# Even-layer residual tiles in the odd layer's buffers, normed rows loaded two steps ahead, and first gates between key pieces

## The chip, the cores and the metric

The kernel runs on one core of a Trainium2 chip. A core has a matrix engine (TensorE, PE in the profile), three engines for elementwise work (VectorE, ScalarE and GpSimd: DVE, ACT and POOL) and a queue engine (SyncE, SP) that here issues nearly all DMAs. Each runs its own list of instructions in order; an instruction starts when the semaphores that it waits for have been raised. The metric is the device time of one execution in microseconds. A time for a version is the median of its timed runs; the profile is of one further execution.

## The reference

The program is one inference step of a two-layer decoder over 2048 prompt tokens and 32 decode tokens (8 sequences of 4), with D = 1024. Layer 0 (even) runs HGRN2 heads and forgetting-attention heads side by side and ends in one output projection; layer 1 (odd) is a gated linear attention (GLA). Cut to the part that matters here:

```
x  = x + concat(o_a, o_b) @ w_out_even           # end of layer 0, residual add
h  = rmsnorm(x, norm_odd)                        # rows of layer 1
q, k, v, g, r = split(h @ w_in_odd)              # 512, 512, 1024, 1024, 16 columns
log_f = log_sigmoid(r @ w_gate + b_gate) / 16    # per key column
o, S  = gated_linear(q * 128**-0.5, k, v, log_f, S0)
x  = x + (head_rmsnorm(o) * silu(g)) @ w_out_odd
return rmsnorm(x, final_norm), ...
```

## The kernel before, in words

Products run in three f16 terms (high times high, high times low, low times high; `mm3`, L583 to L585), so that each f32 operand is first split in two f16 parts by the elementwise engines. The activations of one half of the tokens lie in one tile `act`; half 0 has 1024 prompt tokens and the 32 decode tokens (written 1024 or "few" in names), half 1 the other 1024.

The work of PE is a row of *units*, each a weight block of 256 columns times one half of the tokens. `phase_odd` (L1940) makes them: units 0 to 3 are the even layer's output projection on half 0, units 4 to 7 the same on half 1 (`out_units`, L1787); units 8 to 10 are the odd layer's values, query-and-key, and output gate of head 0 on half 0 (`odd_half`, L1824), and so on. `staged` (L1201) runs a unit and, between its pieces, fetches and splits the weights of the next three.

An out unit goes over token tiles of 128 in pairs (`proj_tm`, L596): 48 matmuls into one PSUM buffer `pt_o` (tag `pj`, three buffers), and then `ev` (L1796) loads the residual rows into a tile `xo` (L1802), adds them to the product on DVE (L1803) and stores the sum to the scratch tensor `x1d` (L1805). A name such as xo0112 means layer 0, half 1, column block 1, token tile 2.

The normed rows of the odd layer are made by `norm_store` (L510), tile by tile of 128 rows: load from `x1d` into `x1r` (L521), sum of squares on ACT (`nsq`, L527), a scale on DVE (`rst_n`, L406) and its power on POOL (`rsr_n`, L408), the gain on POOL (L529), the split in f16 parts on ACT and DVE (L534, L535), and the store to `xs` (L536). Half 0's rows are worked between the pieces of units 4 to 7 (`mux`, L2058: the two generators advance at a fixed ratio). Afterwards `norm_fetch` (L547) loads `xs` transposed into `act`, where the columns that unit 7 has read are free.

Buffers are named by a tag and handed round in turn, so a tile waits for the last use of the tile that had its buffer before. Those that matter (L1947 to L1952): `yr`, two, holds raw attention outputs and `x1r`; `c2`, four, is shared with `th` and holds `xo`, the squares `nsq` and small temporaries; `c4`, six, holds q, k, f and u of the odd layer and lies idle until unit 9; `v8`, two, holds the odd layer's values and lies idle until unit 8.

In unit 9 (`mk_qk`, L1884) three query pieces come first, then `gate` (L1888), which issues its three small matmuls `zC` (L1893, also tag `pj`) in one go with ACT and DVE work on each (L1895, L1896) and four operations on the whole row (L1898 to L1901), then three key pieces.

The order of each engine's list is not that of the code alone: the program is built by a scheduler that simulates a timeline and places each instruction where the simulation has it start, so that a moved load also moves its neighbours on DVE, ACT, POOL and SP.

Of the kernel before, what the change touches and what calls it, by code (L numbers as in the profile page):

```python
# [8 lines left out]
F32 = mybir.dt.float32  # L9
# [5 lines left out]
AF = mybir.ActivationFunctionType  # L15
# [4 lines left out]
P = 128  # L20
D = 1024
KT = D // P
T = 2048
HALF = 1024
DB, DS = 8, 4
TS = DB * DS
# [97 lines left out]
class Kern:  # L124
# [382 lines left out]
    def few_first(tiles):  # L507
        return tiles[8:] + tiles[:8]

    def norm_store(self, pool, hf, tiles, gain):  # L510


        nc = self.nc
        todo = self.few_first(self.ttiles(hf))
        fly = {}

        def load(x):
            c0, n = todo[x]
            fly[x] = [y[:n] for y in tiles(c0)]
            dc = T if c0 >= HALF else hf * HALF + c0  # L520
            nc.sync.dma_start(fly[x][0], self.x1d[dc : dc + n])  # L521

        def norm(x):
            (c0, n), xt = todo[x], fly[x][0]
            sq = pool.tile([P, D], BF16, tag="th", name=f"nsq{c0}")
            ss = pool.tile([P, 1], F32, tag="nss", name=f"nss{c0}")
            nc.scalar.activation(sq[:n], xt, AF.Square, accum_out=ss[:n])  # L527
            fly[x].append(self.rstd(pool, ss[:n], [n, 1], D, f"n{c0}"))
            nc.gpsimd.tensor_tensor(xt, xt, gain[:n], ALU.mult)  # L529

        def split(x):
            (c0, n), (xt, t, r) = todo[x], fly.pop(x)
            dc = T if c0 >= HALF else hf * HALF + c0
            nc.scalar.activation(t[:, 0], xt, AF.Copy, scale=r)  # L534
            nc.vector.scalar_tensor_tensor(t[:, 1], xt, r, t[:, 0], ALU.mult, ALU.subtract)  # L535
            nc.sync.dma_start(self.xs[dc : dc + n], t.rearrange("p x d -> p (x d)"))  # L536

        for x in range(len(todo) + 2):
            if x > 1:
                split(x - 2)  # L540
            if x < len(todo):
                load(x)
            if 0 < x <= len(todo):
                norm(x - 1)
            yield 1000

    def norm_fetch(self, act, hf):  # L547
# [1239 lines left out]
    def out_units(self, hf, layer, act, wpool, wp, pps, x2=None, done=None):  # L1787

        nc, i = self.nc, self.i
        w = i[("w_out_even", "w_out_odd")[layer]][0]  # L1790

        def mk(u):
            cs = slice(u * 256, (u + 1) * 256)
            undo = [self.kcol()] + ([self.kcol()] if layer == 0 and hf == 0 else [])

            def ev(ps, g, cnt, m):  # L1796
                c0 = self.ttiles(hf)[g][0]
                c = undo[-1 if m < P else 0][:m]
                if x2 is None:
                    t = wp.tile([P, 2, 256], F32, tag="c2", name=f"xo{layer}{hf}{u}{g}")  # L1800
                    src = self.rows(hf, c0, m * cnt, layer == 0)[:, cs].rearrange("(g p) d -> p g d", g=cnt)
                    nc.sync.dma_start(t[:m, :cnt], src)  # L1802
                    nc.vector.scalar_tensor_tensor(t[:m, :cnt], ps, c, t[:m, :cnt], ALU.mult, ALU.add)  # L1803
                    dst = self.rows(hf, c0, m * cnt, False)[:, cs].rearrange("(g p) d -> p g d", g=cnt)
                    nc.sync.dma_start(dst, t[:m, :cnt])  # L1805
                else:
                    for j in range(cnt):
                        d = x2[g + j][:m, cs]
                        nc.vector.scalar_tensor_tensor(d, ps[:, j], c, d, ALU.mult, ALU.add)
                        if done:  # L1810
                            done(u, g + j, x2[g + j], cs)
                        if layer == 0 and u == 3:
                            nc.sync.dma_start(self.rows(hf, c0 + j * P, m, False), x2[g + j][:m])

            return (self.half_unit(wpool, pps, w, [(u * 256, 256)], f"o{layer}{u}", f"o{layer}{hf}{u}",
                                   also=list(zip(undo, (self.sy[layer], self.sy[2]))),
                                   raw=("yr", 256) if (hf, layer, u) == (0, 0, 0) else ("wr", WU),
                                   scaler="pool" if (hf, layer, u) == (0, 0, 0) else None),
                    lambda W: self.proj_tm(pps, act, W, hf, ev, f"o{layer}{hf}{u}", pairs=not done or u < 3))

        return [mk(u) for u in range(4)]


    def odd_half(self, hf, act, wpool, wp, pps, S):  # L1824
        nc, i, o = self.nc, self.i, self.o
        w = i["w_in_odd"][0]
        n = self.ncols(hf)
        q, f, k, v, vs, sg = {}, {}, {}, {}, {}, {}
# [4 lines left out]
        def c4(nm):  # L1833
            return wp.tile([P, HALF + TS], F32, tag="c4", name=nm)

        def unit(n, h, run):
            nm, cols = self.odd_cols(h)[n]
            return (self.half_unit(wpool, pps, w, cols, f"{nm}{h}", f"{nm}{hf}{h}"), run)

        def undo(nm):  # L1840
            return self.scales[nm][:, 2:3]
# [42 lines left out]
        def mk_qk(h):  # L1884
            def run(W):
                nm = f"C{hf}{h}"

                def gate():  # L1888
                    f[h], u = c4("f" + nm), c4("u" + nm)
                    ff = f[h]  # L1890
                    for c0, m in self.segs(hf):
                        ps = pps.tile([P, 512], F32, tag="pj", name=f"z{nm}{c0}")
                        nc.tensor.matmul(ps[:, :m], self.wg[:, h * P : (h + 1) * P], rTs[0][:, c0 : c0 + m],  # L1893
                                         start=True, stop=True)
                        nc.scalar.activation(ff[:, c0 : c0 + m], ps[:, :m], AF.Abs, bias=self.bgla[:, h : h + 1])  # L1895
                        nc.vector.tensor_scalar(u[:, c0 : c0 + m], ps[:, :m], self.bgla[:, h : h + 1], 0.0,  # L1896
                                                ALU.add, ALU.min)
                    nc.scalar.activation(ff[:, :n], ff[:, :n], AF.Exp, scale=-1.0)  # L1898
                    nc.scalar.activation(ff[:, :n], ff[:, :n], AF.Ln, bias=1.0)
                    nc.vector.tensor_tensor(ff[:, :n], u[:, :n], ff[:, :n], ALU.subtract)  # L1900
                    nc.scalar.activation(ff[:, :n], ff[:, :n], AF.Exp, scale=1.0 / 16)  # L1901

                q[h], k[h] = c4("q" + nm), c4("k" + nm)
                c = undo(f"Cqk{h}")
                if hf == 0:
                    nc.vector.tensor_scalar(self.q_undo[h], c, SCALE, None, ALU.mult)
                yield from self.proj_fm(pps, act, W, 0, P, hf, lambda ps, c0, m: nc.scalar.activation(
                    q[h][:, c0 : c0 + m], ps, AF.Copy, scale=self.q_undo[h]), nm + "q")
                gate()
                yield Z_C  # L1910
                yield from self.proj_fm(pps, act, W, P, P, hf, lambda ps, c0, m: nc.scalar.activation(
                    k[h][:, c0 : c0 + m], ps, AF.Copy, scale=c), nm + "k")

            return unit(1, h, run)

        def mk_g(h):
# [23 lines left out]
    def phase_odd(self):  # L1940
        tc, nc, i, o = self.tc, self.nc, self.i, self.o
# [3 lines left out]
        with pool("act2", side="right") as ap, pool("w2", side="right") as w0, pool("yr2", side="right") as y0, \  # L1945
                ExitStack() as late:
            raws = Pool(None, {"wr": 3})  # L1947
            wpool = Pool(w0, {"w": 3}, Pool(y0, {"yr": 2}), raws)
            c2s = Pool(None, {"c2": OC2, "th": "c2"})
            wp = Pool(None, {"c4": OC4, "sam": 1, "pd": 1, "kt": 2, "y": OY, "vp": 2, "v8": 2, "vs": 2, "rT": 1,  # L1950
                            "ss": 2, "rs_t": 2, "rs_r": 2, "sg": 3, "rt": 3, "rh": 3, "nss": 2, "gn": 1}, c2s)
            pps = Pool(None, {"pj": 3, "gr": 2, "st": 1, "o": 2})  # L1952
            S = []
            act = self.alloc_act(ap)
# [39 lines left out]
            def load(pieces):  # L1994
                for p in pieces[:2]:
                    p[0]()
                return pieces

            def split(pieces, loaded=2):
                for j, p in enumerate(pieces):  # L2000
                    for step in p[(1 if j < loaded else 0):]:
                        step()
# [42 lines left out]
            grow = self.gain_row(wp.tile([P, D], F32, tag="gn", name="grow"), i["norm_odd"][0], self.sx_odd)  # L2045
# [4 lines left out]
            def prep(hf):  # L2050

                def tiles(c0):
                    t = wpool.tile([P, KT, 256], F32, tag="yr", name=f"x1r{hf}{c0}").rearrange("p k t -> p (k t)")
                    return t[:, :D], t[:, D:].bitcast(F16).rearrange("p (x d) -> p x d", x=2)

                return self.norm_store(wp, hf, tiles, grow)

            drain(mux(prep(0), 11500.0, dense(4, 8), 84000.0))  # L2058
            fetched(11)
            self.norm_fetch(act, 0)  # L2060
# [100 lines left out]
```

## Time and profile before

| | us |
|---|---|
| median of 3 timed runs | 2394.37 (2386.42 to 2399.36) |
| profiled execution, its own time | 2385.88 |
| span of the profiled execution | 2384.2 |
| PE busy | 2273.3 |
| DVE, ACT, POOL busy | 1397.2, 1092.9, 815.8 |

In the profile's rows a bracket such as `[3.54 <-DVE xo L1803]` gives the time that the engine stood idle before the row, and the instruction that ended the wait. `PEclk` in a table by stretches is the share of full clock that TensorE was granted. On the span's time axis units 0 to 7 lie between about 1306 and 1497 us, unit 9 begins in the stretch 1520 to 1540. Lines such as L1803 are lines of the kernel before; in the changed kernel the same instructions stand a few lines lower (L1803 is L1807, L1802 is L1806, L1805 is L1809).

### The profile page before, as it was taken

The numbers are of one execution on the slowest core, as the hardware profiler recorded it, in microseconds if no ns is written. First come the engines' busy times: TensorE is split into PE (matmuls) and PEld (weight loads), VectorE is DVE, ScalarE is ACT, GpSimd is POOL, SyncE is SP. The second block draws the span as 40 slices with busy tenths as digits, with TensorE's granted clock in tenths as the row PEclk, the third lists the DMA queues.
The fourth block names the chain that finished last, engine by engine and source line by source line (L and its number), as shares of the span: only waits on it lengthen the run. The fifth ranks groups of instructions, "written<-read, shape, count | busy, mean of one in ns | idle before, by whom it ended". The sixth has DMA issues, their size and how long they took to land. (4 is left out here: it accounts for less than half of the span.)

```text
span 2384.2 us, 58245 instructions
## 1 busy us (share of the span) xinstructions
PE 2273.3 (95%) x23124; PEld 1617.0 (68%) x23124; DVE 1397.2 (59%) x3231; ACT 1092.9 (46%) x2379; POOL 815.8 (34%) x858
## 2 busy tenths in 40 slices
PE   6999999999999999999999998999899999999998
PEld 5667667864655876655446887777677676666887
DVE  7566566536654638566767444266675655557554
ACT  5334343333333226556667443446545535545333
POOL 1233324112212325234456344043552422322223
PEclk9999999999999999999999999999999999999999
DMA  6221334764441266776874767623233431115453
GB/s 199 63 86 60 93 111 138 193 167 139 144 130 55 78 203 232 241 254 204 267 237 134 248 201 226 158 77 120 83 112 97 114 104 60 43 59 160 154 191 150
DMA packets 358003, 344.89 MB, mean 145 GB/s; under 512 B 90993, under 2 KB 300722, under 8 KB 357730
## 3 DMA queue, kind: packets, MB, share of 16 engines
q1 hardware_dynamic: 356226, 336.64, 46.2%
q8 instruction: 182, 2.98, 0.5%
q0 software_dynamic: 1504, 4.52, 0.5%
q14 instruction: 91, 0.75, 0.1%
HBM read 248.73 MB, written 79.63 MB: 138 GB/s over the span
## 5 line engine op out<-in xcount | busy, mean ns | idle before, releaser
L583 PE MATMUL pt_o<-w_o,act 128*128 128x256 f16 x1024 | 282.9, 276 | 11.6 <-DVE xo L1803 9.2
L585 PE MATMUL pt_o<-w_o,act 128*128 128x256 f16 x1024 | 283.0, 276 | 4.8 <-DVE act L1766 4.1
L584 PE MATMUL pt_o<-w_o,act 128*128 128x256 f16 x1024 | 282.9, 276 | 0.0
L583 PEld LDWEIGHTS <-act 128*128 128x128 f16 x2304 | 227.7, 99 | 40.2 <-DVE xo L1803 3.8
L584 PEld LDWEIGHTS <-act 128*128 128x128 f16 x2304 | 227.7, 99 | 38.1 <-issue 7.6
L585 PEld LDWEIGHTS <-act 128*128 128x128 f16 x2304 | 227.9, 99 | 37.3 <-DVE act L1766 5.0
L749 POOL TENSOR_TENSOR kA<-kA,fA 128x512 f32<-128x512 f32 (+1 forms) x56 | 78.9, 1409 | 191.3 <-PE gl_A L715 142.7
L583 PE MATMUL pt_Cv<-w_Cv,act 128*128 128x256 f16 (+1 forms) x512 | 141.4, 276 | 0.0
L584 PE MATMUL pt_Cv<-w_Cv,act 128*128 128x256 f16 (+1 forms) x512 | 141.4, 276 | 0.0
L585 PE MATMUL pt_Cv<-w_Cv,act 128*128 128x256 f16 (+1 forms) x512 | 141.2, 276 | 0.0
L749 POOL TENSOR_TENSOR kC<-kC,fC 128x512 f32<-128x512 f32 (+1 forms) x56 | 83.5, 1492 | 151.8 <-PE gl_C L715 100.4
L1374 ACT ACTIVATE L<-L,nm,kc 128x512 f32<-128x512 f32 (+3 forms) x160 | 118.2, 741 | 37.5 <-DVE nm L1372 33.4
L1382 POOL TENSOR_SCALAR L<-L,nm 128x512 f32<-128x512 f32 (+3 forms) x160 | 98.8, 631 | 63.0 <-DVE nm L1378 22.1
L1409 ACT ACTIVATE th<-pt 128x512 f16<-128x512 f32 (+3 forms) x159 | 80.4, 527 | 61.3 <-PE pt L1402 60.3
L1410 DVE TENSOR_TENSOR tl<-pt,th 128x512 f16<-128x512 f32 (+3 forms) x159 | 94.5, 609 | 21.4 <-ACT th L1409 20.4
L1402 PE MATMUL pt<-ident,L 128*128 128x128 f32 x544 | 91.3, 280 | 6.5 <-POOL L L1382 3.8
L1402 PEld LDWEIGHTS pt<-ident,L 128*128 128x128 f32 x544 | 67.0, 144 | 32.8 <-DVE tl L1410 8.9
L1526 PEld LDWEIGHTS pkt<-ident,pgcache_fox_k 128*128 128x128 f32 x512 | 57.5, 141 | 42.6 <-issue 25.1
L1526 PE MATMUL pkt<-ident,pgcache_fox_k 128*128 128x128 f32 x512 | 74.7, 278 | 7.4 <-DVE kts L1530 5.3
L1855 ACT ACTIVATE vC<-pt_Cv,kc 128x512 f32<-128x512 f32 (+1 forms) x40 | 23.9, 599 | 123.2 <-PE pt_Cv L585 123.2
L583 PE MATMUL pt_Av<-w_Ai,act 128*128 128x256 f16 x256 | 71.1, 278 | 0.5 <-ACT act L578 0.5
L584 PE MATMUL pt_Av<-w_Ai,act 128*128 128x256 f16 x256 | 70.9, 277 | 0.4 <-DVE w_Ai L349 0.4
(952 smaller groups left out, 6752.9 us busy)
## 6 DMA issues: line engine op xcount, KB each, us to landing
pgcache_fox_k<-in_cache_fox_k SPq DMA_DIRECT2D x128, 256.0 KB, 4.3
pgcache_fox_v<-in_cache_fox_v SPq DMA_DIRECT2D x128, 256.0 KB, 4.1
yr<-yT SPq DMA_DIRECT2D x16, 1024.0 KB, 6.9
x1d<-xo SPq DMA_DIRECT2D x48, 256.0 KB, 3.6
wr_Aqf<-in_w_in_even SPq DMA_DIRECT2D x64, 128.0 KB, 3.3
wr_o<-in_w_out_even SPq DMA_DIRECT2D x32, 256.0 KB, 6.1
xo<-in_x_prompt SPq DMA_DIRECT2D x32, 256.0 KB, 3.4
wr_Cv<-in_w_in_odd SPq DMA_DIRECT2D x32, 256.0 KB, 3.8
```

Source lines behind the costliest of these rows:

```text
L583: nc.tensor.matmul(ps, lh[0], rh[0], start=first, stop=False)
L584: nc.tensor.matmul(ps, lh[0], rh[1], start=False, stop=False)
L585: return nc.tensor.matmul(ps, lh[1], rh[0], start=False, stop=last)
L749: nc.gpsimd.tensor_tensor(kv[:, :, 0], kv[:, :, 0], t1.to_broadcast([P, nb, w]), ALU.mult)
L1374: self.last_exp = nc.scalar.activation(lt[:, :w], lt[:, :w], AF.Exp, bias=nm[:, 0:1], scale=ib, accum_out=nm[:, 2 + j : 3 + j])
L1382: nc.gpsimd.tensor_scalar(lt[:, :w], lt[:, :w], nm[:, 1:2], 2.0**14, ALU.mult, ALU.mult)
L1402: nc.tensor.transpose(pt[:, w : w + P], rows[b][s // 4][0][:, (s % 4) * P : (s % 4 + 1) * P], self.ident)
L1409: nc.scalar.activation(th[:, a:w], pt[:, a:w], AF.Copy),
L1410: nc.vector.tensor_tensor(tl[:, a:w], pt[:, a:w], th[:, a:w], ALU.subtract)))
L1526: nc.tensor.transpose(pk[:, j * P : (j + 1) * P], pgs[j][:, h * P : (h + 1) * P], self.ident)
L1855: r = nc.scalar.activation(v[h][:, g : g + cnt], ps[:, :, :256], AF.Copy, scale=c)
```

## The change

Three parts. (1) In `ev`, the residual tiles of layer 0 come from tag `c4` (six buffers) in place of `c2` (four, shared with `nsq`); those of layer 1 stay. (2) `norm_store` has a parameter `lead`, the number of steps by which a row tile's load runs ahead of its norm: 2 for half 0, 1 for half 1 (which is the old order). For half 0 every second row tile (128, 384, 640, 896) is taken from `v8` in place of `yr`, so that there are four buffers. (3) In `mk_qk` the gate of head 0 is a generator that yields between its segments, and its steps are taken between the key pieces; the other heads' gates run through at once, as before.

```diff
@@ norm_store @@
-        for x in range(len(todo) + 2):
-            if x > 1:
-                split(x - 2)
-            if x < len(todo):
-                load(x)
-            if 0 < x <= len(todo):
-                norm(x - 1)
+        for x in range(-lead, len(todo) + 1):
+            if x > 0:
+                split(x - 1)
+            if x + lead < len(todo):
+                load(x + lead)
+            if 0 <= x < len(todo):
+                norm(x)
             yield 1000
@@ out_units, ev @@
-                    t = wp.tile([P, 2, 256], F32, tag="c2", name=f"xo{layer}{hf}{u}{g}")
+                    if layer:
+                        t = wp.tile([P, 2, 256], F32, tag="c2", name=f"xo{layer}{hf}{u}{g}")
+                    else:
+                        t = wp.tile([P, HALF + TS], F32, tag="c4", name=f"xo{layer}{hf}{u}{g}")[:, :512].rearrange(
+                            "p (g d) -> p g d", g=2)
@@ mk_qk @@
-                    for c0, m in self.segs(hf):
+                    for x, (c0, m) in enumerate(self.segs(hf)):
+                        if x and h == 0:
+                            yield
...
-                gate()
+                gates = gate()
+                next(gates, None)
                 yield Z_C
-                yield from self.proj_fm(pps, act, W, P, P, hf, lambda ps, c0, m: nc.scalar.activation(
-                    k[h][:, c0 : c0 + m], ps, AF.Copy, scale=c), nm + "k")
+                for x in self.proj_fm(pps, act, W, P, P, hf, lambda ps, c0, m: nc.scalar.activation(
+                        k[h][:, c0 : c0 + m], ps, AF.Copy, scale=c), nm + "k"):
+                    next(gates, None)
+                    yield x
@@ phase_odd, prep @@
-                    t = wpool.tile([P, KT, 256], F32, tag="yr", name=f"x1r{hf}{c0}").rearrange("p k t -> p (k t)")
+                    p, tag = (wp, "v8") if hf == 0 and c0 // P % 2 else (wpool, "yr")
+                    t = p.tile([P, KT, 256], F32, tag=tag, name=f"x1r{hf}{c0}").rearrange("p k t -> p (k t)")
...
-                return self.norm_store(wp, hf, tiles, grow)
+                return self.norm_store(wp, hf, tiles, grow, 1 + (hf == 0))
```

How it moves instructions is shown at three places. First the list of DVE in units 5 and 6 (half 1). Here rst_n384 is the scale of row tile 384, x1r0384 its split, and xo0112 the add that empties a PSUM buffer of unit 5. Before:

```order
L406 TENSOR_SCALAR rst_n256_20865<-nss256_20863 128x1
L1803 SCALAR_TENSOR_TENSOR xo0110_20778<-pt_o0110_20729,kc_67,xo0110_20778 128x512
L535 SCALAR_TENSOR_TENSOR x1r0256_20794<-x1r0256_20794,rsr_n256_20867 128x1024
L406 TENSOR_SCALAR rst_n384_20943<-nss384_20941 128x1
L1803 SCALAR_TENSOR_TENSOR xo0112_20853<-pt_o0112_20804,kc_67,xo0112_20853 128x512
L535 SCALAR_TENSOR_TENSOR x1r0384_20860<-x1r0384_20860,rsr_n384_20945 128x1024
L1803 SCALAR_TENSOR_TENSOR xo0114_20919<-pt_o0114_20870,kc_67,xo0114_20919 128x512
L406 TENSOR_SCALAR rst_n512_21071<-nss512_21069 128x1
L1803 SCALAR_TENSOR_TENSOR xo0116_20997<-pt_o0116_20948,kc_67,xo0116_20997 128x512
```

And after, from the same xo0110 on:

```order
L1807 SCALAR_TENSOR_TENSOR xo0110_20767<-pt_o0110_20718,kc_67,xo0110_20767 128x512
L535 SCALAR_TENSOR_TENSOR x1r0384_20849<-x1r0384_20849,rsr_n384_21062 128x1024
L406 TENSOR_SCALAR rst_n640_21256<-nss640_21254 128x1
L535 SCALAR_TENSOR_TENSOR x1r0512_20927<-x1r0512_20927,rsr_n512_21128 128x1024
L1807 SCALAR_TENSOR_TENSOR xo0112_20842<-pt_o0112_20793,kc_67,xo0112_20842 128x512
L535 SCALAR_TENSOR_TENSOR x1r0640_21055<-x1r0640_21055,rsr_n640_21258 128x1024
L406 TENSOR_SCALAR rst_n768_21325<-nss768_21323 128x1
L1807 SCALAR_TENSOR_TENSOR xo0114_20908<-pt_o0114_20859,kc_67,xo0114_20908 128x512
L535 SCALAR_TENSOR_TENSOR x1r0768_21121<-x1r0768_21121,rsr_n768_21327 128x1024
L406 TENSOR_SCALAR rst_n896_21389<-nss896_21387 128x1
L1807 SCALAR_TENSOR_TENSOR xo0116_20986<-pt_o0116_20937,kc_67,xo0116_20986 128x512
```

The row tiles have moved forward by about three tiles against the adds: where 384 stood beside xo0112, now 512 and 640 do. In the whole list the row tiles 128 to 896 now end between xo0104 and xo0120 (unit 6); before, the last, x1r0896, stood behind xo0124.

Second, SP's list at the start of the out units. Here yr... are the raw attention outputs (1 MB each) that become `act`, wr_o... weights, xo0000 the first residual load. Before:

```order
L330 DMA wr_o001_19308<-in_w_out_even 128x2x256 x4
L1802 DMA xo0000_19398<-in_x_prompt 128x2x256
L1752 DMA yr000512_19313<-yT0_76 128x8x256
L330 DMA wr_o002_19402<-in_w_out_even 128x2x256 x4
L1802 DMA xo0002_19469<-in_x_prompt 128x2x256
L330 DMA wr_o003_19473<-in_w_out_even 128x2x256 x4
L1802 DMA xo0004_19527<-in_x_prompt 128x2x256
L1802 DMA xo0006_19593<-in_x_prompt 128x2x256
L1752 DMA yr000768_19325<-yT0_76 128x8x256
L1752 DMA yr0010240_19337<-yT0_76 128x8x32
```

After:

```order
L330 DMA wr_o002_19402<-in_w_out_even 128x2x256
L1752 DMA yr000512_19313<-yT0_76 128x8x256
L330 DMA wr_o002_19402<-in_w_out_even 128x2x256 x3
L330 DMA wr_o003_19473<-in_w_out_even 128x2x256 x4
L1752 DMA yr000768_19325<-yT0_76 128x8x256
L1752 DMA yr0010240_19337<-yT0_76 128x8x32
L1806 DMA xo0000_19398<-in_x_prompt 128x2x256
L1806 DMA xo0002_19469<-in_x_prompt 128x2x256
L1806 DMA xo0004_19527<-in_x_prompt 128x2x256
L1806 DMA xo0006_19593<-in_x_prompt 128x2x256
```

The first four residual loads have moved behind the last two loads of raw outputs; POOL's scaling of the norm's gain row (`grow`, L458) has likewise moved behind POOL's splits of those two.

Third, ACT's list in unit 9, its three kinds of rows for the query (qC00), the gate (fC00) and the key (kC00). Before:

```order
L1907 ACTIVATE qC00_21856<-pf_C00q704_21920,kc_67 128x352
L1895 ACTIVATE fC00_21957<-zC000_21959,bgla_766 128x352
L1895 ACTIVATE fC00_21957<-zC00352_21963,bgla_766 128x352
L1895 ACTIVATE fC00_21957<-zC00704_21967,bgla_766 128x352
L1898 ACTIVATE fC00_21957<-fC00_21957 128x1056
```

After:

```order
L1913 ACTIVATE qC00_21856<-pf_C00q704_21920,kc_67 128x352
L1901 ACTIVATE fC00_21957<-zC000_21959,bgla_766 128x352
L1918 ACTIVATE kC00_21857<-pf_C00k0_21963,kc_67 128x352
L1901 ACTIVATE fC00_21957<-zC00352_21989,bgla_766 128x352
L1918 ACTIVATE kC00_21857<-pf_C00k352_21993,kc_67 128x352
L1901 ACTIVATE fC00_21957<-zC00704_22019,bgla_766 128x352
L1904 ACTIVATE fC00_21957<-fC00_21957 128x1056
```

The gate's segments alternate with the key pieces, on PE as on ACT. The same is done in unit 21 (half 1, two segments). Elsewhere the lists stand as before.

More of the change, by code (lines that the diff above doesn't have):

```diff
@@ L508, in few_first, with norm_store @@
         return tiles[8:] + tiles[:8]
-    def norm_store(self, pool, hf, tiles, gain):
+    def norm_store(self, pool, hf, tiles, gain, lead):
         nc = self.nc
```

## The prediction, made before the changed kernel was run

> **What bounds the kernel now.** I read the table of engines first.
>
> ```profile
> span 2384.2 us, 58245 instructions
> PE 2273.3 (95%) x23124; PEld 1617.0 (68%) x23124; DVE 1397.2 (59%) x3231; ACT 1092.9 (46%) x2379; POOL 815.8 (34%) x858
> ```
>
> PE is the bound, so only its idle time and its clock can be won. Next, the table by stretches around the change (out units from 1306 to 1497, unit 9 from about 1525).
>
> ```profile
> core 0: us, PE busy (x) PEld busy (x) DVE busy (x) ACT busy (x) POOL busy (x), PEclk, DMA share, GB/s
> 1300.00:1340.00 40.00, 36.05 (x331) 30.64 (x330) 21.36 (x31) 26.62 (x50) 23.27 (x19) 0.96 0.96 300
> 1340.00:1440.00 100.00, 99.93 (x965) 88.44 (x963) 40.21 (x55) 38.97 (x62) 35.91 (x24) 1.00 0.68 210
> 1440.00:1460.00 20.00, 16.46 (x137) 13.87 (x135) 5.10 (x8) 6.56 (x10) 6.40 (x5) 0.91 0.66 221
> 1460.00:1480.00 20.00, 17.17 (x143) 14.60 (x141) 8.41 (x9) 6.16 (x9) 9.40 (x7) 0.91 0.80 264
> 1480.00:1500.00 20.00, 17.15 (x141) 14.46 (x140) 7.23 (x8) 3.41 (x5) 5.11 (x4) 0.91 0.91 201
> 1520.00:1540.00 20.00, 16.76 (x119) 10.40 (x119) 7.40 (x19) 15.48 (x26) 2.33 (x2) 0.94 0.36 119
> 1540.00:1560.00 20.00, 20.00 (x133) 12.97 (x131) 4.48 (x4) 9.14 (x15) 2.72 (x2) 0.98 0.20 53
> ```
>
> PE is full from 1340 to 1440; then three stretches of 20 us each lose about 3 us of work and 0.09 of the clock. The waits of PE from 1290 to 1560 name what they wait for (total, times, longest):
>
> ```profile
> PE pt_o L583 <- DVE xo L1803: 9.2, 3, 3.5
> PE zC L1893 <- ACT qC L1907: 2.6, 1, 2.6
> PE pt_o L583 <- ACT act L1762: 1.5, 1, 1.5
> PE pS_o L627 <- DVE sam_o L622: 1.1, 1, 1.1
> PE pt_o L585 <- POOL act L1763: 0.6, 1, 0.6
> PE pf_C00k L583 <- DVE uC L1896: 0.6, 1, 0.6
> ```
>
> The 9.2 us are the three losses: PE has no PSUM buffer until DVE has added a residual. Why DVE is late, the timeline of SP, ACT, DVE and PE shows at the first of them:
>
> ```profile
> 1435.59 0.39 SPq L521 DMA_DIRECT2D x1r<-x1d  x1
> 1442.14 1.06 ACT L527 ACTIVATE nsq<-x1r 128x1024 bf16<-128x1024 f32 x1 [3.72 <-DMA x1r<-x1d]
> 1443.32 0.15 DVE L406 TENSOR_SCALAR rst_n<-nss 128x1 f32<-128x1 f32 x1 [3.58 <-ACT nsq L527]
> 1443.43 0.75 DVE L1803 SCALAR_TENSOR_TENSOR xo<-pt_o,kc,xo 128x512 f32<-128x512 f32 x1
> 1444.24 0.28 PE L583 MATMUL pt_o<-w_o,act 128*128 128x256 f16 x1 [3.54 <-DVE xo L1803]
> ```
>
> The add stands behind rst_n384 in DVE's list, that waits for nsq, and nsq for the load of its row tile, which was issued only at 1435.59, when its buffer came free. The waits from 1400 to 1500 confirm whose load it is:
>
> ```profile
> ACT nsq L527 <- DMA x1r<-x1d: 18.9, 6, 5.0
> DVE xo L1803 <- PE pt_o L585: 7.9, 2, 4.5
> DVE xo L1803 <- DMA xo<-in_x_sample: 0.5, 1, 0.5
> SPq L1802 <- ACT nsq L527: 16.3, 7, 4.6
> ```
>
> The adds hardly ever wait for their own residual (0.5 us); the row tiles do wait for theirs (18.9). The residual loads do wait, for a buffer that nsq holds (16.3), but they land in time.
>
> **The cost part by part.** *Row tiles in four buffers.* The present rhythm of row tiles and of pairs:
>
> ```profile
> 1424.79 1.06 ACT L527 ACTIVATE nsq<-x1r 128x1024 bf16<-128x1024 f32 x1 [4.96 <-DMA x1r<-x1d]
> 1477.68 1.06 ACT L527 ACTIVATE nsq<-x1r 128x1024 bf16<-128x1024 f32 x1 [4.02 <-DMA x1r<-x1d]
> 1492.13 0.75 DVE L1803 SCALAR_TENSOR_TENSOR xo<-pt_o,kc,xo 128x512 f32<-128x512 f32 x1 [3.38 <-PE pt_o L585]
> 1497.37 0.75 DVE L1803 SCALAR_TENSOR_TENSOR xo<-pt_o,kc,xo 128x512 f32<-128x512 f32 x1 [4.49 <-PE pt_o L585]
> x1r<-x1d SPq DMA_DIRECT2D x10, 512.0 KB, 4.4
> xs<-x1r SPq DMA_DIRECT2D x8, 512.0 KB, 3.9
> L529 POOL TENSOR_TENSOR x1r<-x1r,grow 128x1024 f32<-128x1024 f32 (+1 forms) x9 | 21.6, 2400 | 40.0 <-ACT nsq L527 33.6 <-DMA xs<-x1r 6.5
> L408 POOL TENSOR_TENSOR rsr_n<-rst_n,mhalf 128x1 f32<-128x1 f32 (+1 forms) x9 | 6.4, 715 | 0.0
> ```
>
> From nsq of tile 128 (1424.79) to that of tile 896 (1477.68) are six tiles: 52.9/6 = 8.8 us per tile, so a buffer's turn is 2 × 8.8 = 17.6 us. Four buffers give 17.6/4 = 4.4 us. No engine forbids that: POOL, the fullest, has 2.40 + 0.72 = 3.1 us per tile. A pair of PE takes 1497.37 − 1492.13 = 5.24 us. In the new list of DVE seven tiles (128 to 896) end between xo0104 and xo0120, six pairs apart: 6 × 5.24 = 31.4 us, and PE can run two pairs ahead on its three buffers, 10.5 more: 41.9. Seven tiles at 4.4 take 30.8, so PE isn't held and the 9.2 us go. The row tiles then end before unit 7 begins; what is late next is nothing that I find before the transposes, which wait for PE itself.
>
> *The clock.* In the three stretches with a gap it is 0.91, so 0.09 × 20 = 1.8 us are lost in each; at 1.00 elsewhere. With the gaps gone I take these 5.4 us too. [...] The three waits sum to 9.2 with a longest of 3.5, so the other two average 2.85, and their stretches stand at 0.91 nevertheless: I go by the rows.
>
> *Residual tiles in c4.* Same DMAs, same adds: nothing on the path in 1400 to 1500, because the loads already land in time there; the cover is the 5.24 us per pair times several buffers. It frees `c2` for nsq. Two waits are new and covered: unit 8's values now follow row tiles in `v8`, and unit 9's q, k, f and u follow residuals in `c4`, both stored before PE reaches these units. It costs something only at the start, where the first four loads now stand behind two loads of raw outputs:
>
> ```profile
> 1310.02 1.22 SPq L1802 DMA_DIRECT2D xo<-in_x_prompt  x2
> 1311.56 2.86 SPq L1752 DMA_DIRECT2D yr<-yT  x2
> 1322.41 2.91 POOL L458 TENSOR_SCALAR grow<-grow,kc 128x1024 f32<-128x1024 f32 x1 [8.39 <-DMA grow<-in_norm_odd]
> 1325.30 3.69 POOL L1763 TENSOR_TENSOR act<-yr,act 128x512 f16<-128x512 f32 x4
> 1323.97 0.28 PE L583 MATMUL pt_o<-w_o,act 128*128 128x256 f16 x1 [1.51 <-ACT act L1762]
> ```
>
> PE is ready for its fourth pair at 1323.97 − 1.51 = 1322.5. The gain's row held POOL there, ahead of its splits of the last raw outputs (1325.30), for which PE waited three times: 1.5 + 1.1 + 0.6 = 3.2 us, and 0.04 × 40 = 1.6 of clock, 4.8 together. In the new lists four residual loads (1 MB at 300 GB/s, some 3 us) no longer precede the raw outputs, and grow stands behind the splits. Against it, the first residual can't be issued before the second raw load, 1311.56 + 2.86 = 1314.4 or a little sooner. Landing as the row tiles' loads do (4.4) it is there at 1318.8, in time; with twice that, 1323.2, the add ends 1.5 us after PE is ready, and behind it in DVE's list stand the next unit's weight splits, so that PE may wait as long again: I bound the loss at 3. Between −4.8 and +3 I take half the gain, 2.4.
>
> *Gate between key pieces.* PE waited 2.6 + 0.6 us in unit 9 because `zC` needs a PSUM buffer that the third query piece holds, and its evacuation on ACT stood behind a weight's scaling that waited for its DMA:
>
> ```profile
> 1534.31 0.72 ACT L354 ACTIVATE wr_Cv<-wr_Cv,kc 128x512 f32<-128x512 f32 x1 [1.15 <-DMA wr_Cv<-in_w_in_odd]
> PE pf_C10k L583 <- ACT qC L1907: 1.9, 1, 1.9
> ```
>
> Now one `zC` and a key piece come before that buffer is needed: 24 matmuls of 352 columns, by the pair's 48 of 256 in 5.24 us some 3.6 us. That covers the 2.6, and both waits go: 3.2. The clock's share is 0.06 × 20 + 0.02 × 20 = 1.6. The gate's operations on the whole row end two key pieces later, but the recurrence that reads them begins only after unit 10. The second row above is the same wait in unit 21; there other work of the scheduler moved too, so between 0 and 1.9 I take 1.
>
> Sum: 9.2 + 5.4 + 2.4 + 3.2 + 1.6 + 1.0 = 22.8 us. The profiled execution took 2385.9 (span 2384.2), which gives 2363; it was 8.5 us below the median of the runs shown, 2394.4, so for a median I expect 2394.4 − 22.8 = 2371.6.
>
> **Rivals.** All as medians.
> (a) *Two buffers in effect.* If the row tiles keep their 8.8 us, because SP takes loads and stores in order and each tile's load queues behind a store that waits for DVE, seven tiles take 61.6 against 41.9: 19.7 us lost, 14.6 now. With 4.8 won at unit 9 it is even, 2394. For it speaks that SP's list still alternates loads with waiting stores; against it, that 128 and 384 are now loaded ahead of tile 1024.
> (b) *Slower.* The same mechanism with longer landings: more row and residual loads are in flight together where DMA already moves 201 to 264 GB/s. If load and store land 2 us later each, a two-buffer turn is 21.6 us, a tile 10.8, seven take 75.6: 33.7 lost, 19.1 more than now, 14 after unit 9's gain: 2409. It decides above 8.8 us per tile.
> (c) *The clock falls for another reason than gaps that short.* Then the clock's share of two of the three gaps, of unit 9 and half of that of the start stays: 1.8 + 1.8 + 1.6 + 0.8 = 6, and the time is 2378. Against it is that the stretches below 1.00 lie at gaps and the full one has none. [...]
>
> **How the numbers follow.** The forecast has 0.72. At the best the start gives 4.8 and unit 21 1.9, 3.3 us more than taken; at the worst the start costs 3 and unit 21 gives nothing, 6.4 less; with some 5 us either way, since the three runs spread over 13, its own range is 2363 to 2383. (a) has 0.13, (b) 0.07, (c) 0.08. The range begins at 2362 and reaches up to 2387, which takes in (c) and the part of (a) where some of the gain comes. What a measurement can tell from no change is about 0.5%, 12 us: faster is below 2382.4. That holds for nearly all of the forecast and (c), 0.77; (a) with the weak ends of both gives 0.15 for the same; (b) and a little of (a) 0.08 for slower.
>
> **What would show it.** Right: no wait of pt_o for xo from 1400 to 1490, PEclk 1.00 there, nsq about 4 to 5 us apart with few waits for x1r's load, zC without a wait, units 0 to 7 some 15 us shorter. Wrong: nsq still 8 to 9 us apart; pt_o waiting for xo at a new place, above all around 1322 with the add waiting for its residual; the clock at 0.91 without a gap; or a new wait of pt_Cv on the transposes after 1480.

## The result, and the profile after

The changed kernel took 2370.4 us (median of 4 runs, 2367.9 to 2374.4), the kernel before in runs beside it 2392.1: a ratio of 0.991, with a 95% interval from 0.989 to 0.993. In a later group the same pair took 2369.7 and 2384.9, a ratio of 0.994 (0.992 to 0.995). The profiled execution took 2367.9, its span is 2366.2, against 2384.2 before: 18.0 less. Two single executions of the experiments below, the profiled one of p3 (3118.7 us) and one of p23 (3298.8 us), ran at a mean clock of 0.70 and 0.65; they are in no ratio, and p3's stages are not read.

The table of engines and the stretches of the kernel after (columns as before; the stretches now lie some 14 us earlier in the work at the end of the out units):

```profile
span 2366.2 us, 58225 instructions
PE 2268.5 (96%) x23124; PEld 1613.5 (68%) x23124; DVE 1398.6 (59%) x3231; ACT 1092.6 (46%) x2379; POOL 818.9 (35%) x858
```

```profile
core 0: us, PE busy (x) PEld busy (x) DVE busy (x) ACT busy (x) POOL busy (x), PEclk, DMA share, GB/s
1300.00:1340.00 40.00, 37.69 (x358) 32.79 (x357) 21.82 (x31) 26.92 (x51) 21.63 (x18) 1.00 1.03 335
1340.00:1440.00 100.00, 96.18 (x925) 84.57 (x922) 43.80 (x58) 43.07 (x69) 46.43 (x30) 1.00 0.71 224
1440.00:1460.00 20.00, 18.68 (x172) 16.73 (x172) 11.14 (x14) 8.02 (x11) 10.87 (x7) 1.00 0.81 273
1460.00:1480.00 20.00, 20.00 (x186) 17.94 (x184) 5.71 (x6) 2.38 (x4) 2.72 (x2) 1.00 0.80 200
1480.00:1500.00 20.00, 20.00 (x177) 17.15 (x175) 5.69 (x21) 5.75 (x11) 2.32 (x2) 1.00 1.03 213
1520.00:1540.00 20.00, 19.78 (x140) 12.88 (x138) 6.29 (x7) 13.52 (x20) 2.78 (x2) 1.00 0.11 25
```

PE is full and at full clock from 1460 on, where three stretches of 20 us had lost about 3 us each. But the stretch from 1340 to 1440, full before, now lacks 3.8 us, and POOL's work in it rose from 35.9 to 46.4: the row tiles, and with them the waits, moved forward. The waits of PE from 1290 to 1560:

```profile
PE pt_o L583 <- DVE xo L1807: 5.1, 4, 2.8
PE pt_o L584 <- POOL w_o L356: 1.5, 2, 0.8
PE pf_C00k L583 <- DVE uC L1902: 0.2, 1, 0.2
PE pt_o L585 <- POOL act L1763: 0.2, 1, 0.2
```

The wait of `zC` is gone, the start keeps 1.5 + 0.2, but the adds still hold PE for 5.1 of the 9.2 us. The chain behind the longest of these waits, from the timelines of POOL, ACT, DVE and PE in order of time:

```profile
1430.54 2.87 POOL L356 TENSOR_TENSOR w_o<-wr_o,w_o 128x512 f16<-128x512 f32 x2
1433.37 3.33 POOL L529 TENSOR_TENSOR x1r<-x1r,grow 128x1024 f32<-128x1024 f32 x1
1436.66 0.55 POOL L408 TENSOR_TENSOR rsr_n<-rst_n,mhalf 128x1 f32<-128x1 f32 x1
1437.24 1.15 ACT L534 ACTIVATE x1r<-x1r,rsr_n 128x1024 f16<-128x1024 f32 x1 [3.92 <-POOL rsr_n L408]
1438.42 2.18 DVE L535 SCALAR_TENSOR_TENSOR x1r<-x1r,rsr_n 128x1024 f16<-128x1024 f32 x1 [3.87 <-ACT x1r L534]
1440.53 0.74 DVE L1807 SCALAR_TENSOR_TENSOR xo<-pt_o,kc,xo 128x512 f32<-128x512 f32 x1
1441.32 0.28 PE L583 MATMUL pt_o<-w_o,act 128*128 128x256 f16 x1 [2.76 <-DVE xo L1807]
```

Where the add stood behind `rst_n`, which waited for a load, it now stands behind a row tile's split, which waits for POOL, and POOL worked the next unit's weights in between. The groups of POOL by line, 1400 to 1490 (busy time, mean ns of one, idle before):

```profile
L529 POOL TENSOR_TENSOR x1r<-x1r,grow 128x1024 f32<-128x1024 f32 (+1 forms) x9 | 22.3, 2474 | 13.8 <-ACT nsq L527 13.8
L408 POOL TENSOR_TENSOR rsr_n<-rst_n,mhalf 128x1 f32<-128x1 f32 (+1 forms) x9 | 9.5, 1051 | 0.0
```

The power takes 1.05 us where it took 0.72, the gain 2.47 where it took 2.40. The power and DVE's split of a row took longer here where POOL and DVE worked side by side. Of the nine powers the four with no split on DVE beside them took 0.54 to 0.58 us, the five with one 1.03 to 1.58; in the kernel before it was seven, of 0.55 to 0.58, and two, of 1.02 and 1.53. And DVE's split of a row, 1.28 us where POOL stood idle as it began, took 2.18 in the chain above, where it began under the next row's gain on POOL:

```profile
1437.17 2.35 POOL L529 TENSOR_TENSOR x1r<-x1r,grow 128x1024 f32<-128x1024 f32 x1
```

It ended 1.08 us after that gain, and so, within 0.01, did each of the four splits that began under a gain. So some 0.9 us (2.18 − 1.28) of the longest wait goes with POOL and DVE at work side by side, though no run takes the two apart. The loads hardly matter any more, as ACT's waits from 1400 to 1490 show:

```profile
ACT x1r L534 <- POOL rsr_n L408: 16.7, 7, 3.9
ACT nsq L527 <- DMA x1r<-x1d: 2.6, 3, 1.7
```

The row rhythm is that of `nsq`, first and last of seven tiles in ACT's timeline:

```profile
1412.84 1.04 ACT L527 ACTIVATE nsq<-x1r 128x1024 bf16<-128x1024 f32 x1
...
1447.42 1.06 ACT L527 ACTIVATE nsq<-x1r 128x1024 bf16<-128x1024 f32 x1
```

From `nsq` of tile 128 to that of tile 896: (1447.42 − 1412.84)/6 = 5.8 us per tile, where it was 8.8.

By stages, from the first matmul of each in the trace (units 0 to 7; 8; 9; on to unit 21; 21; the rest), in us:

| | 0 to 7 | 8 | 9 | to 21 | 21 | rest |
|---|---|---|---|---|---|---|
| before | 191.3 | 24.0 | 27.8 | 325.9 | 28.3 | 481.0 |
| after | 179.1 | 24.0 | 23.2 | 326.3 | 26.2 | 483.2 |

So −12.2, −4.6 and −2.0 (28.26 to 26.24) where the change is at work; +0.4, +2.2 and −1.8 ahead of unit 0 are stages that it doesn't touch.

### The profile page after: what moved, and what is told of

Same layout as the page of the kernel before. It is cut to its first block, busy times and chain, and to the rows that moved or that the text cites. A ratio compares the mean times of both kernels' runs of the same rounds, so it can differ in the third digit from the quotient of the medians.

```text
span 2366.2 us, 58225 instructions
## 1 busy us (share of the span) xinstructions
PE 2268.5 (96%) x23124; PEld 1613.5 (68%) x23124; DVE 1398.6 (59%) x3231; ACT 1092.6 (46%) x2379; POOL 818.9 (35%) x858
## 5 line engine op out<-in xcount | busy, mean ns | idle before, releaser
L1807 DVE SCALAR_TENSOR_TENSOR xo<-pt_o,kc,xo 128x512 f32<-128x512 f32 x48 | 35.8, 748 | 62.6 <-PE pt_o L585 62.3
L583 PE MATMUL pt_Av<-w_Ai,act 128*128 128x256 f16 x256 | 71.0, 277 | 0.5 <-ACT act L578 0.5
```

Of the source, the lines that this page charges most:

```text
L583: nc.tensor.matmul(ps, lh[0], rh[0], start=first, stop=False)
```

## The experiments

Ratios are to the kernel before, timed on the same chip in the same group. "Wait" is what PE waits in units 4 to 7 for residual adds (`pt_o` for `xo`, and for `rst_n` where that stood there alone); stages are as above.

| run | ratio (95%) | 0 to 7 | wait | 8 | 9 |
|---|---|---|---|---|---|
| before | 1 | 191.3 | 9.2 | 24.0 | 27.8 |
| p1: part 1 alone | 0.998 (0.996 to 0.999) | 191.0 | 13.7 | 24.0 | 25.6 |
| p2: part 2 alone | 1.000 (0.999 to 1.001) | 193.7 | 12.8 | 24.0 | 28.7 |
| p3: part 3 alone | 0.996 (0.994 to 0.997) | not read | not read | not read | not read |
| p23: parts 2 and 3 | 0.997 (0.996 to 0.999) | 194.2 | 12.9 | 24.0 | 25.3 |
| lead2only: two buffers | 0.996 (0.995 to 0.997) | 190.2 | 12.1 | 24.0 | 23.7 |
| p2sq | 0.997 (0.995 to 0.998) | 183.2 | 6.1 | 24.0 | 32.2 |
| nogain | 0.989 (0.987 to 0.991) | 177.0 | 3.5 | 24.0 | 24.3 |
| gaindve | 0.992 (0.990 to 0.994) | 184.7 | 10.0 | 24.0 | 24.2 |
| after5: the change again | 0.994 (0.992 to 0.995) | 180.2 | 5.0 | 24.0 | 23.2 |
| ia13 | 0.995 (0.993 to 0.997) | 182.2 | 6.7 | 24.0 | 27.1 |
| ia145 | 0.993 (0.992 to 0.995) | 179.5 | 5.4 | 24.0 | 24.5 |
| rp145 | 0.992 (0.990 to 0.993) | 176.2 | 2.6 | 30.2 | 24.4 |

**The parts alone.** p1, p2 and p3 are the kernel before with one part of the diff each, p23 the changed kernel without the residual tiles in `c4`.

> The kernel before with the first part alone: residual tiles of the even units in the other buffers. Theory (the loads of the row tiles hold the adds): the three waits of pt_o for xo between 1440 and 1500 stay near 9.2 us with the clock at 0.91 beside them; only the start near 1325 changes, by -4.8 to +3, so a time of 2387 to 2395 against 2392. Rival (residual loads that wait 16.3 us for a buffer that nsq holds are what held the adds): the waits fall to under 4 us and the time to about 2380.

> The kernel before with the second part alone: row tiles loaded two steps ahead in four buffers. Theory (the row tiles' loads): nearly all of the gain of units 0 to 7 is here, rows 5.8 us apart as with the whole change, waits for xo about 5 us in place of 9.2, clock 1.00 there, about -10 us against before. Rival (the first part is needed, since nsq and the residuals take their buffers from the same set): rows more than 8 us apart, gain under 4 us.

> The kernel before with the third part alone: first gates between key pieces. Theory: unit 9 loses its wait of zC (2.6 + 0.6 us) and 1.6 of the clock, unit 21 some 2, and nothing changes between 1300 and 1500: -5 to -7 us against before. Rival (what unit 9 won came from an earlier arrival at it, not from the gates): unit 9 stays at 27.8 us, change within 1.5 us.

> The changed kernel without its first part (residual tiles stay where they were). Theory (the parts add up and the first does nothing past the start): the start near 1325 loses its 4.8 us as before the change, the rest as with the whole change: 2371 to 2376. Rival (the first part carries some of the second's gain, because nsq takes its buffers from the residuals' set): 2380 or more, with new waits of nsq for an add.

Part 3 has three prices: 0.996 by itself, 10 us against the 5 to 7 expected; p23 against p2 0.3%, 6 us; and 4.0 us in units 9 and 21 between two profiles compared further down (lead2only against p1). What made p3's figure the largest is not shown. Part 1 alone wins the start (0.7 + 0.8 + 0.3 us of waits there, clock 1.00), and loses nearly as much again at the adds: their waits grow to 13.7 us, which neither theory nor rival had, and the time, 2386.0, comes 1 us below the range expected. But part 2 alone, on which the forecast had put the whole gain of units 0 to 7, gives nothing: here the rival was right, and p23 (2385.0 us, with `nsq` waiting 31.7 us for stores of residuals) says the same. ACT's waits from 1400 to 1500, in p2 and then in p1:

```profile
ACT nsq L527 <- DMA x1d<-xo: 31.6, 8, 10.6
ACT nsq L527 <- DMA x1r<-x1d: 7.9, 1, 7.9
```

```profile
ACT nsq L527 <- DMA x1r<-x1d: 22.7, 6, 7.6
```

In p2 the rows do land early, but `nsq` writes its squares, which nobody reads, into a buffer that it shares with the residual tiles, and that comes free only when a residual's store (`x1d<-xo`) has landed. In p1 these buffers are free and the load is late as before. Each part takes away one of two waits in the same place, and the other ends last. The profile before had a sign of it that the prediction didn't show, one wait of `nsq` for a residual's store in ACT's waits from 1400 to 1500:

```profile
ACT nsq L527 <- DMA x1d<-xo: 2.8, 1, 2.8
```

**The shared buffer by itself.** p2sq is p2 with the squares written elsewhere; the residual tiles stay in `c2`.

```diff
-            sq = pool.tile([P, D], BF16, tag="th", name=f"nsq{c0}")
+            sq = fly[x][1][:, 0] if hf == 0 else pool.tile([P, D], BF16, tag="th", name=f"nsq{c0}")[:n]
```

> The kernel before with the second part, and the squares of nsq written into the unused half of their own row tile in place of a buffer of the set that the residual tiles use. Theory (in the second part alone, nsq waits 31.6 us for buffers of the residuals' set until their stores have landed, and that alone cancels the four row buffers): that wait is gone, rows come 5 to 6 us apart, units 0 to 7 shorten by about 9 us as far as they did with both parts (12.2 less the start's 3), time about 2381 against 2390. Rival (the residual loads' new place is what counts, not nsq's buffer): no gain over the second part alone, 2388 to 2392, with the waits for xo still above 9 us.

The squares no longer wait for a residual's store, but for their row's load (ACT's waits from 1400 to 1500):

```profile
ACT x1r L527 <- DMA x1r<-x1d: 12.8, 5, 7.9
```

Units 0 to 7 shorten by 8.0 against before and by 10.5 against p2, about the 9 expected; rows come 6.3 us apart, a little over the 5 to 6 expected. So it was `nsq`'s buffer, not the residual loads' place. (The edit also leaves all four buffers of `c2` to the residuals and small temporaries, but in p2 only one wait of DVE from 1400 to 1500, of 2.0 us, ends with a residual load, so that these loads were not what held the adds there.) The total came to 2384.8 (2381 expected), because unit 9 took 32.2 us in this order, with `zC` waiting 4.2 in place of 2.6 before, a new wait of 1.4 ahead of it, and the clock at one half for 6.8 us of it (PEclk 0.83 from 1520 to 1540), where it was 3.4 before. Whether part 3 would take that away was not run.

**Lead or buffers.** lead2only is the changed kernel with all row tiles in `yr`.

```diff
-                    p, tag = (wp, "v8") if hf == 0 and c0 // P % 2 else (wpool, "yr")
-                    t = p.tile([P, KT, 256], F32, tag=tag, name=f"x1r{hf}{c0}").rearrange("p k t -> p (k t)")
+                    t = wpool.tile([P, KT, 256], F32, tag="yr", name=f"x1r{hf}{c0}").rearrange("p k t -> p (k t)")
```

> The changed kernel with row tiles loaded two steps ahead but in the two old buffers. Theory (a load needs a free buffer, so that the lead alone does little): rows 8 us or more apart, waits for xo 9 to 14 us in units 0 to 7, 5 to 9 us slower than the changed kernel, so 2375 to 2380. Rival (the lead carries the gain): within 2 us of the changed kernel.

The buffers carry it: 12.1 us of waits without them. With two buffers the lead moves nothing: from unit 0 until past unit 21 the trace of lead2only has the rows of POOL and SP in the same order as that of p1, and those of DVE and ACT but for the gates of part 3. With four buffers, whether a lead of one would do as well was not run. Since lead2only is thus p1 and part 3, the two price part 3: unit 9 takes 23.7 in place of 25.6 (the wait of `zC`, 2.1 us, is gone) and unit 21 26.2 in place of 28.4 (its wait of 2.0 is gone), with the clock at 1.00 in unit 9 of both.

**What holds the 5.1 us that are left.** Three tries: the gain left out, the gain on DVE, and the order of DVE's list changed.

```diff
 nogain:
-            nc.gpsimd.tensor_tensor(xt, xt, gain[:n], ALU.mult)
+            if hf == 1:
+                nc.gpsimd.tensor_tensor(xt, xt, gain[:n], ALU.mult)
 gaindve:
+            (nc.vector if hf == 0 else nc.gpsimd).tensor_tensor(xt, xt, gain[:n], ALU.mult)
 ia145 (ia13 with 13000):
+            with self.tc.issue_after(self.add.ins) if hf == 0 else nullcontext():
                 nc.vector.scalar_tensor_tensor(t[:, 1], xt, r, t[:, 0], ALU.mult, ALU.subtract)
...
-            drain(mux(prep(0), 11500.0, dense(4, 8), 84000.0))
+            drain(mux(prep(0), 14500.0, dense(4, 8), 84000.0))
```

> The changed kernel with the gain's multiplication on POOL left out in the first half of the tokens (a part of the computation is missing). Theory (the 5.1 us of waits for xo that are left come from POOL: 2.4 us of gain per row tile, with the split of the next unit's weights between them): the waits for xo between 1395 and 1450 fall under 1 us, 4 to 6 us less than the changed kernel's 2370. Rival (what is left comes from the place of the adds behind the row splits in DVE's list, or from the loads): 3 us or more of these waits stay.

> The changed kernel with the gain's multiplication of the first half's row tiles on DVE in place of POOL. Theory (POOL holds the row tiles): POOL's 2.4 us per tile go, DVE gets 1.1 to 2.2 (the nearest rows: its split of a row takes 1.3 to 2.2), the waits for xo fall from 5.1 to under 2 us, time 3 to 5 us below the changed kernel's 2370. Rival (DVE is held just as much, since the adds stand in its list behind the new multiplications): the waits for xo stay at 5 or grow to 10, 2370 to 2376.

> The changed kernel, with DVE's split of each row tile of the first half queued behind the add that stands ahead of it in the code, and the row tiles spread further (14500 in place of 11500 in the ratio), so that at most one split stands between two adds. Theory (the 5.1 us left are adds that stand in DVE's list behind splits that still wait for POOL): the waits for xo fall under 2 us, units 0 to 7 take 175 to 177 us in place of 179.1, time 2 to 5 us under the changed kernel's. Rival (the row tiles end too late for it): unit 8 waits for its activations after 1480, and the time is 0 to 10 us above the changed kernel's.

> The same with 13000, so that the row tiles come somewhat earlier and two splits stand together once. Theory: waits for xo between 1 and 4 us, 1 to 4 us under the changed kernel's time. Rival (place in the list makes no difference): 5 us of waits as in the changed kernel, and its time.

> The changed kernel once more, timed beside the two others. Both theories: 2370 within 3 us, waits for xo in units 0 to 7 of 4 to 6 us.

Without the gain 3.5 us of waits stay (under 1 expected), so POOL's multiplication holds only a part of them; units 0 to 7 are 2.1 us shorter than in the changed kernel. On DVE it doubles the waits, as the rival had it. With the splits spread by ia145 the waits are smaller (none over 1.5) and more, with the same sum; ia13 has 6.7, 4.1 of it at one place, and both theories are off for it. PE's waits from 1300 to 1560 in ia145 (lines two higher), and then DVE's from 1395 to 1500:

```profile
PE pt_o L585 <- DVE xo L1809: 5.4, 5, 1.5
```

```profile
DVE rst_n L407 <- ACT nsq L528: 25.5, 8, 7.5
```

The adds, no longer behind a split, stand behind `rst_n` again, where DVE waits 25.5 us for `nsq` (9.0 from 1400 to 1490 in the changed kernel). So the last run adds one edit to ia145: in half 0 `rst_n` is computed on POOL, which leaves DVE no wait for `nsq`.

```diff
-        nc.vector.tensor_scalar(t, ss, 1.0 / n, EPS, ALU.mult, ALU.add)
+        (first or nc.vector).tensor_scalar(t, ss, 1.0 / n, EPS, ALU.mult, ALU.add)
```

> The kernel with the spread splits (14500), and in the first half also the scale rst_n on POOL in place of DVE. Theory (with the splits spread, the 5.4 us of waits for xo that came back are adds that stand in DVE's list behind rst_n, which waits 25.5 us for nsq): the waits for xo fall under 2 us, units 0 to 7 take 175 to 177 us, time 2 to 4 us under the changed kernel's, a ratio of about 0.992 to the kernel before where the changed kernel had 0.991 to 0.994. Rival (POOL, with another operation per row tile, holds the splits just as long, and the adds behind these): waits for xo of 4 us or more, and the changed kernel's time or up to 5 us above it.

PE's waits from 1300 to 1560, and the longest of those in unit 8 in PE's timeline:

```profile
PE pt_Cv L585 <- DMA act<-xs: 4.2, 2, 3.3
PE pt_o L585 <- DVE xo L1809: 2.6, 2, 1.4
```

```profile
1493.37 0.29 PE L585 MATMUL pt_Cv<-w_Cv,act 128*128 128x272 f16 x1 [3.33 <-DMA act<-xs]
```

SP's last store of a row tile, and the first transpose behind it:

```profile
1485.38 0.42 SPq L538 DMA_DIRECT2D xs<-x1r  x1
1485.89 3.13 SPq L555 DMA_TRANSPOSE act<-xs  x1
```

The waits halve and units 0 to 7 take 176.2, as the theory had it, so the adds' place in DVE's list is shown to hold about half of what was left. (The 2 us aimed at were missed by 0.6.) But the row tiles now end later (the last `nsq` at 1466.4, where it was 1447.4 in the changed kernel), their transposes stand behind their stores on SP, and unit 8 waits 4.2 us for its activations, with the clock at 0.91 from 1480 to 1500: 30.2 against 24.0. What units 0 to 7 won is given back. None of the versions that compute everything is shown to be faster than the changed kernel.

## Why the prediction was right, and where it was not

The time was right: 2370.4 against 2371.6, inside the range. Its own sum was too large: 22.8 forecast, against 18.0 between the two profiled executions, 21.7 between the medians of the first group and 15.2 in the later one. So that the time came within 1.2 us is in part luck: the 2394.4 that it starts from is a median of three runs that spread over 13 us; with one more run it is 2392.1, and the same sum gives 2369.3.

- *PE and its waits bound the kernel; the adds wait behind row tiles that are late.* Right, and p2sq shows it from another side: no residual tile was moved there and units 0 to 7 shortened by 8 us.
- *"The 9.2 us go".* This step failed: 4.1 went. The prediction took 4.4 us per tile from four turns of a 17.6 us buffer, and no limit on POOL above 3.1. Measured is 5.8 per tile: POOL's gain and power took 2.47 + 1.05 = 3.5, with 2.87 of weight splits in a row between two tiles, and the adds wait for the splits in DVE's order. It counted what an engine works in the mean and not what stands between two tiles in its list. A rhythm of 5.8 is also just inside the 41.9/7 = 6.0 at which the prediction's own slack ends, so a mean rhythm could not show these waits: the tiles come in bursts.
- *"Residual tiles in c4": nothing on the path in 1400 to 1500.* Wrong in its price. The prediction saw that it frees `c2` for `nsq` and set nothing for it. Without it part 2 wins nothing (193.7 and 194.2 against 179.1 and 180.2 with it): the two parts win together what neither wins alone. The total came right because both were in the change.
- *The start, half of 4.8.* Nearer the whole: 3.2 us of waits became 1.5 + 0.2 and the clock stood at 1.00, so about 3.1. p1 shows the same by itself.
- *The clock in the out units, 5.4.* It went, but not because the gaps did: four of up to 2.8 us stayed, and what differed in these traces was the place of a gap (last section). In after5 one of them cost 1.7 again. Rival (c) took such gaps to be too short for the clock; no run shows a length that decides by itself: a gap of 2.76 us left the clock at 1.00 in the kernel after and was followed by 3.41 us at 0.50 in after5.
- *Unit 9, 4.8; unit 21, 1.0.* 4.6 and 2.0, so unit 21 gave a little more than the upper end, 1.9. The waits of both are part 3's, as lead2only against p1 shows (1.9 and 2.1 us). The clock's share in unit 9 is not: p1, without part 3, stood at 1.00 there with `zC` waiting 2.1. And part 3 does not always take the whole wait of `zC`: 1.4 of it are left in p23.
- *What is late next.* The prediction found nothing before the transposes. In the changed kernel the adds are still next; the transposes come after them, and rp145 met them.
- Rival (a), two buffers in effect, comes near to what part 2 does without part 1, but for another cause: the row tiles are 9.3 us apart there (`nsq` of tile 128 at 1426.45, of tile 896 at 1482.51 in p2), by way of the squares' buffer and not of SP's order.
- Rival (b), longer landings, did not come: from 1290 to 1520 the row tiles' loads take 5.2 us to land in the median, where they took 4.4, and the stores 3.7, where they took 3.9; it needed 2 us more of each. `nsq` waits 2.6 us for loads in place of 18.9.

Open: what holds the rest of the 5.1 us, and how much of it goes with POOL and DVE at work side by side. Half goes with the splits spread and `rst_n` off DVE, and 1.6 with POOL's gain left out; both at once was not tried, nor were the waits of the start for the weight split on POOL (1.5).

## What to carry to other kernels

When a stall has a late load as its last wait, look at every other thing that the waiting instruction needs, its output buffer too: a scratch result that nobody reads can hold a whole pipeline if it shares buffers with tiles that wait for a store (`nsq`, 31.6 us of waits in p2). Price such parts of a change together or not at all, since a wait is put down to what ended last (`nsq` before: 18.9 us for loads and 2.8 for stores; with part 2 alone: 7.9 and 31.6). And a mean time per tile doesn't prove that an in-order engine won't be held (5.8 us here where 6.0 were to suffice, and 5.1 us of waits): read what stands in its list between two of them.

## What the runs showed of the clock

The clock fell in whole stretches of about 3.4 us at one half, which is the 0.91 of a 20 us window. I had expected it to follow gaps. In these traces it followed neither their presence nor their length alone, but the place of the gap on a grid: in the clock records of before and after each change of the clock lies on a grid with a step of 3.413 us (within 0.01), and where the grid lies against the program differed from execution to execution (by 1.6 us between before and after, by 2.0 us between after and after5). Three gaps from PE's timeline, each with the windows of the grid that it touches and the one behind. PE's busy time is the first number after the comma, PEclk the third from the right. First the kernel after:

```profile
1441.32 0.28 PE L583 MATMUL pt_o<-w_o,act 128*128 128x256 f16 x1 [2.76 <-DVE xo L1807]
```

```profile
1436.68:1440.09 3.41, 1.89 (x18) 1.45 (x15) 1.67 (x1) 1.15 (x1) 3.41 (x4) 1.00 0.98 331
1440.09:1443.51 3.42, 2.19 (x20) 1.97 (x21) 2.46 (x5) 2.19 (x3) 1.12 (x2) 1.00 1.05 401
1443.51:1446.92 3.41, 3.41 (x34) 3.05 (x32) 0.73 (x3) 0.65 (x1) 2.72 (x2) 1.00 1.03 315
```

The same kernel in after5:

```profile
1438.77 0.39 PE L583 MATMUL pt_o<-w_o,act 128*128 128x256 f16 x1 [2.76 <-DVE xo L1807]
```

```profile
1434.68:1438.09 3.41, 1.33 (x13) 0.95 (x10) 2.22 (x2) 1.15 (x1) 3.41 (x2) 1.00 0.95 296
1438.09:1441.51 3.42, 2.74 (x13) 1.94 (x14) 2.46 (x4) 2.19 (x3) 1.12 (x2) 0.50 1.03 385
```

And gaindve:

```profile
1434.30 0.27 PE L583 MATMUL pt_o<-w_o,act 128*128 128x256 f16 x1 [3.18 <-DVE xo L1807]
```

```profile
1429.52:1432.93 3.41, 1.60 (x15) 1.28 (x14) 2.23 (x6) 3.05 (x6) 1.64 (x2) 1.00 1.04 391
1432.93:1436.35 3.42, 2.05 (x19) 1.84 (x19) 3.42 (x4) 3.42 (x6) 3.42 (x3) 1.00 0.87 293
1436.35:1439.76 3.41, 3.35 (x31) 2.85 (x30) 3.41 (x4) 2.14 (x5) 0.34 (x1) 1.00 0.36 96
```

The gap of 2.76 us is cut in two by the grid in the kernel after, so that PE is busy for 0.55 and 0.64 of the two windows, and the clock stays. In after5 most of it falls in one window, busy for 0.39, and the next stands at one half. The longer gap of gaindve leaves 0.47 and 0.60, and the clock stays. From 1300 to 1560 us before and after have 148 windows of the grid at full clock: the 5 in which PE was busy for 0.23 to 0.39, all of them in before, were each followed by one at half clock, and the 143 others, busy for 0.55 or more, never. The three gaps of the kernel before left 0.32, 0.35 and 0.37. In later stages of the two, with other kinds of matmul, windows busy for 0.45 to 0.53 were followed by either. There a gap of 1.85 us in the kernel after, with thin work around it, left 0.46 and brought the clock down:

```profile
1674.39 0.50 PE L800 MATMUL stS_C<-hl_C,kpad_C 96*128 96x256 f32 x2 [1.85 <-DVE s_C L804]
```

```profile
1672.15:1675.56 3.41, 1.56 (x24) 1.00 (x25) 3.25 (x8) 0.00 (x0) 3.41 (x4) 1.00 0.10 32
1675.56:1678.98 3.42, 3.42 (x13) 1.78 (x14) 3.36 (x7) 3.00 (x7) 1.41 (x3) 0.51 0.47 155
```

So the same gap of 2.76 us cost no clock in one execution of the kernel after and 1.7 us (half of 3.41) in another. The 5.4 us that the prediction booked for three gaps are what these gaps cost in that execution, not what such gaps cost each time.
